# Holding the scores back ahead of the last step of the last input chunk, and transposing the first layer's first queries one step later

## The chip, the cores and the metric

The kernel runs on one core of a Trainium2 chip. The metric is the device time of one execution in microseconds (us). Engines are named as in the profile: PE (TensorE's matmuls), PEld (its weight loads), DVE (VectorE), ACT (ScalarE), POOL (GpSimd), SP (the queue that issues most transfers). "L466" is line 466 of the kernel before; in the changed kernel the same line is a few lines further down.

## The reference

The program is a transformer trunk of two layers, 256 tokens by 2048 features, all in float32. Cut to what matters here:

```python
for l in range(2):
    h = rmsnorm(x, norm_mix[l])
    proj = h @ w_in[l]                       # columns of three mixers: A, B, C
    oa = window_attention(qa, ka, va, ...)       # 8 heads, 2 kv heads, +-128 tokens, sink, bias
    ob = neighborhood_attention(qb, kb, vb, ...) # 8 heads, 2-D window, bias
    oc = axial_global_attention(qc, kc, vc, ...) # 16 heads, 4 kv heads, rotary, all tokens
    mix = concat(rmsnorm(oa, ga), rmsnorm(ob, gb), rmsnorm(oc, gc))
    x = x + mix @ w_o[l]
    h = rmsnorm(x, norm_mlp[l])
    u = relu(h @ w_up[l])
    x = x + (u * u) @ w_down[l]
out = rmsnorm(x, norm_final)
```

## The kernel before, in words

**Steps.** All weight matrices are cut into tiles of 128 x 1024 numbers. One tile is one `Step`. The loop at the end of the kernel goes through the steps in order: it issues the load of a tile seven steps ahead (`load`, on SP, into one of five `wraw` buffers), splits a tile two steps ahead into a rounded high part and a low part (`split`: a cast `whi<-wraw` on ACT, L1013, and a subtraction `wlo<-wraw,whi` on DVE, L1014; each fourth pair goes to buffers called `spare`), runs the step's matmuls (`s.mm`, for the projections L466), and then calls `tick()`.

A step of a projection has three matmuls for each product: high by high, high by low, low by high. A wide input step and an output step are 12 matmuls of 512 columns; a step of the narrow chunk `kva` is 24 of 256 columns.

**Order of the steps.** In each layer the input chunks come as `qa, kva, kvc, qc0, qc1, vb, b0, b1`, eight steps each (`kva` four). Then come the output steps, group by group in the order A, C, B: for A 4 column blocks of 2 steps, for C 4 of 4, for B 4 of 2. Then the MLP follows.

**Evacuation.** After the last step of a chunk `proj_evac` copies the two PSUM banks to SBUF on ACT (for `b0`, `b1` at L515, for `qa` at L565) and queues the pieces that come from it.

**Pieces and units.** Attention is done in pieces that are put between the steps. A unit covers four pairs of head and query block and has three pieces: `unit_scores` (eight matmuls into the score banks `S`, L342 and L343; then on DVE for group C a maximum over the scores, L349, for A and B a fused sum and minimum, L356; on ACT the exponentials, L360; on POOL the reciprocal sums, L369, and four scalings, L371), `unit_transp` (eight transposes, L380, split by ACT, L381, and DVE, L382), and `unit_pv` (matmuls with V, L399 or for group B L392, a copy on ACT, L402, and additions on DVE, L412 or L407). There is one set of score banks. Queries and keys are made ready by `q_transposes` (L255, with copies on ACT, L259, and DVE, L262) and `k_transposes` (L271, with copies and two transfers).

After the last unit of a block, `mix_prep` scales the block for the output projection (ACT L422, DVE L423) and adds its squares on POOL into `sqacc` (L426, then two additions at L435). After the last block of a group, `mix_rs` is queued: a small matmul over `sqacc` (L443) and the reciprocal root (DVE L445, POOL L245). The output steps of a group need that result at the end of their first column block.

**The planner.** `add` puts a piece in the list `bgq` with a cost, the pieces it comes after, and a delay. `tick()` advances a clock `cur` by 2.6, goes through the list, and emits each piece whose predecessors are done and whose delay has passed, until a budget of 2.2 is spent. `need` emits pieces from the head of the list until a flag is set. The layer that records the program then places the instructions of neighbouring pieces and steps into each engine's own list, and picks the buffers; each engine works its list strictly in order.

Of the kernel before, what the change touches and what calls it, by code (L numbers as in the profile page):

```python
# [43 lines left out]
def tile_trunk(ctx: ExitStack, tc: tile.TileContext, x_in, xt_in, w_in, w_o, w_up, w_down,  # L44
# [2 lines left out]
    LOOK_LOAD, LOOK_SPLIT, LOOK_PREP, BUDGET = 7, 2, 5, 2.2  # L47
    N_WARM = 8
    D_X, D_S, D_SS, D_T, D_PV, D_QK, D_RQ, D_RK, D_SQ, D_R = 6.0, 6.0, 7.0, 18.0, 6.0, 6.0, 24.0, 16.0, 6.0, 4.0

    cp = ctx.enter_context(tc.tile_pool(name="cp", bufs=1))
    wp = ctx.enter_context(tc.tile_pool(name="wp", bufs=1))
# [103 lines left out]
    last_lo, last_act, last_load = [None], [None], [None]  # L156

    class Piece:
        pass

    def add(fn, cost, after=(), delay=0, front=False):

        p = Piece()
        p.fn, p.cost, p.after, p.delay, p.at, p.done = fn, cost, after, delay, cur[0], None
        bgq.insert(0 if front else len(bgq), p)
        return p

    def emit(p):
        bgq.remove(p)
        cur[0] += p.cost  # L170
        p.done = cur[0]
        p.fn()

    def tick():
        cur[0] += 2.6
        spent = 0.0
        for p in list(bgq):
            if spent and spent + p.cost > BUDGET:
                break
            if any(q.done is None for q in p.after):  # L180
                continue
            t0 = max([q.done + d for q, d in zip(p.after, p.delay)]) if p.after else p.at + p.delay
            if t0 <= cur[0]:
                emit(p)
                spent += p.cost
# [142 lines left out]
    def queue_unit(u, *preps):  # L328

        after = list(preps) + last_s[-1:]  # L330
        sc = add(lambda: unit_scores(u), 0.87, after=after, delay=[D_S] * len(preps) + [D_SS])
        tr = add(lambda: unit_transp(u), 0.87, after=(sc,), delay=(D_T,))
        add(lambda: unit_pv(u), 0.87, after=(tr,), delay=(D_PV,))
        last_s.append(sc)

    def unit_scores(u):
# [36 lines left out]
    def unit_transp(u):  # L373
        u.ph = big(F32R, 2, 512)
        u.pl = big(F32R, 2, 512)
        for kb in range(2):
            ps = tr_bank()
            for s in range(4):
                c = u.col(s)
                nc.tensor.transpose(ps[:, c * P:(c + 1) * P], u.p[:, s, kb * P:(kb + 1) * P], ident)  # L380
            nc.scalar.copy(u.ph[:, kb, :], ps)  # L381
            nc.vector.tensor_sub(u.pl[:, kb, :], ps, f(u.ph[:, kb, :]))  # L382
# [68 lines left out]
    steps = []  # L451

    class Step:


        def __init__(self, src, kk, n, pre, mm, fourth=True, loads=None, prep=None, raw=None, post=None):
            self.src, self.kk, self.n, self.pre, self.mm, self.fourth = src, kk, n, pre, mm, fourth
# [28 lines left out]
    def layer_steps(l):  # L486
        st = {"hT": [None] * 8, "ss": small(8 if l else 4), "mixT": [None] * 8, "sqacc": {}, "rg": {}, "V": {}, "q": {}, "k": {}}
# [22 lines left out]
        def proj_evac(name, banks):  # L510
            r = st["r"]
            if name in ("b0", "b1"):
                qs = big(F32, NT, 512)
                for t in range(NT):
                    nc.scalar.activation(qs[:, t, :], banks[t], AF.Copy, scale=r[:, t:t + 1])  # L515
                qT, kh, kl = big(F32R, 4, 256), big(F32R, 4, 256), big(F32R, 4, 256)
                pq = add(lambda: q_transposes(qs, 0, qT, 0.125), 0.45, delay=D_QK)
                i = int(name[1])
                pk = add(lambda: k_transposes(qs, 2, 2, kh, kl), 0.45, after=(pq,), delay=(2.6,))
                for u in range(2):  # L520
                    queue_unit(b_unit(l, st, 4 * i + 2 * u, qT, kh, kl), pq, pk)
            elif name == "vb":
                V = [big(F32R, NT, 4, 2, 64) for _ in range(2)]
                st["V"]["B"] = V
                for t in range(NT):
                    v_split(banks[t], [(0, 4, V[0]), (256, 4, V[1])], t, r[:, t:t + 1])
            elif name == "kvc":
                raw = mid(F32, NT, 4, 64)
                V = big(F32R, NT, 4, 2, 64)
                st["V"]["C"] = V  # L530
                for t in range(NT):
                    nc.scalar.activation(raw[:, t].rearrange("p h d -> p (h d)"), banks[t][:, 0:256], AF.Copy,
                                         scale=r[:, t:t + 1])
                    v_split(banks[t], [(256, 4, V)], t, r[:, t:t + 1])
                ks = mid(F32, NT, 256)

                def outs(t, a, b):
                    nc.gpsimd.tensor_add(ks[:, t, :].rearrange("p (h d) -> p h d", h=4), a, b)
                rope(raw, 4, "k", l, outs)
                kh, kl = big(F32R, 4, 256), big(F32R, 4, 256)  # L540
                st["k"]["C"] = (kh, kl)
                st["kC"] = add(lambda: k_transposes(ks, 0, 2, kh, kl), 0.45, delay=D_RK)
            elif name in ("qc0", "qc1"):
                raw = big(F32, NT, 8, 64)
                for t in range(NT):
                    nc.scalar.activation(raw[:, t].rearrange("p h d -> p (h d)"), banks[t], AF.Copy,
                                         scale=r[:, t:t + 1])
                qs = big(F32, NT, 512)

                def outs(t, a, b):  # L550
                    nc.gpsimd.tensor_add(qs[:, t, :].rearrange("p (h d) -> p h d", h=8), a, b)
                rq = rope(raw, 8, "q", l, outs)
                i = int(name[2])
                kh, kl = st["k"]["C"]
                for g in range(2):
                    qT = big(F32R, 4, 256)
                    pq = add(lambda g=g, qT=qT: q_transposes(qs, 2 * g, qT, 1.0), 0.45, delay=D_RQ)
                    for qb in range(2):
                        c0 = qb * 8 + 4 * g
                        queue_unit(g_unit(l, st, "C", 2 * i + g, qb, qT, kh, kl, st["V"]["C"],  # L560
                                          rq=rq[:, c0:c0 + 4]), pq, st["kC"])
            elif name == "qa":
                qs = big(F32, NT, 512)
                for t in range(NT):
                    nc.scalar.activation(qs[:, t, :], banks[t], AF.Copy, scale=r[:, t:t + 1])  # L565
                st["q"]["A"], st["qA"] = [], []
                for g in range(2):
                    qT = big(F32R, 4, 256)
                    st["q"]["A"].append(qT)
                    st["qA"].append(add(lambda g=g, qT=qT: q_transposes(qs, 2 * g, qT, 0.125), 0.45, delay=D_QK))  # L570
            else:
                ks = mid(F32, NT, P)
                V = mid(F32R, NT, 2, 2, 64)
                for t in range(NT):
                    nc.scalar.activation(ks[:, t, :], banks[t][:, 0:P], AF.Copy, scale=r[:, t:t + 1])
                    v_split(banks[t], [(128, 2, V)], t, r[:, t:t + 1])
                kh, kl = mid(F32R, 2, 256), mid(F32R, 2, 256)
                pk = add(lambda: k_transposes(ks, 0, 1, kh, kl), 0.3, delay=D_QK)
                for g in range(2):
                    bias = bias_a(g)  # L580
                    for qb in range(2):
                        queue_unit(g_unit(l, st, "A", g, qb, st["q"]["A"][g], kh, kl, V, bias), st["qA"][g], pk)

        ti = 0
        for name in IN_CHUNKS:
            wide = name != "kva"
            nk = 2 if wide else 4
            nst = NKB // nk
            n = 512 if wide else 256
            box = {}  # L590
            for k in range(nst):
                src = w_in[l, ti]
                ti += 1

                def pre(k=k, nk=nk):
                    need((("mix", l), (k * nk + nk - 1) // 2))

                def mm(wh, wl, k=k, nk=nk, nst=nst, n=n, box=box, name=name):
                    if k == 0:
                        box["b"] = [mm_bank(), mm_bank()]  # L600
                    hts = [halves(st["hT"][(k * nk + i) // 2]) for i in range(nk)]
                    mode_b(box["b"], hts, wh, wl, [(k * nk + i) % 2 for i in range(nk)], k == 0, k == nst - 1, n,
                           lo_last=l == 0 and name == IN_CHUNKS[0], by_block=k == 0)
                    if k == nst - 1:
                        proj_evac(name, box["b"])
                steps.append(Step(src, nk, n, pre, mm))


        st["hT2"], st["ss2"] = [None] * 8, small(8)
        i = 0  # L610
# [439 lines left out]
    for i, s in enumerate(steps):  # L1050
# [31 lines left out]
        if i == 11:  # L1082
            with tc.issue_after(last_lo[0]):
                setup_tables()
        tick()
    assert not bgq


# [121 lines left out]
```

## Time and profile before

| what | value |
|---|---|
| median of 3 runs | 2006.74 us (2006.64 to 2006.88) |
| profiled execution | 2007.62 us, span of its instructions 2005.8 us |
| PE busy | 99% of the span |
| DVE, ACT, POOL busy | 80%, 61%, 17% |
| granted TensorE clock, mean | 0.999 |

The span runs from the first to the last instruction; the profiled execution's own time is 1.8 us longer. Times inside the execution are given in microseconds from the span's start. A timeline row reads: start, duration, engine, line, operation, output and input tiles, count; in brackets, where there is one, the idle time of the engine just before and what ended it. The ends of PE rows are modelled and overlap the next row; starts are what to go by.

### The profile page before, as it was taken

The numbers are of one execution on the slowest core, as the hardware profiler recorded it, in microseconds if no ns is written. First come the engines' busy times: TensorE is split into PE (matmuls) and PEld (weight loads), VectorE is DVE, ScalarE is ACT, GpSimd is POOL, SyncE is SP. The second block draws the span as 40 slices with busy tenths as digits, with TensorE's granted clock in tenths as the row PEclk, the third lists the DMA queues.
The fourth block names the chain that finished last, engine by engine and source line by source line (L and its number), as shares of the span: only waits on it lengthen the run. The fifth ranks groups of instructions, "written<-read, shape, count | busy, mean of one in ns | idle before, by whom it ended". The sixth has DMA issues, their size and how long they took to land.

```text
span 2005.8 us, 28051 instructions
## 1 busy us (share of the span) xinstructions
PE 1992.2 (99%) x10206; PEld 1698.6 (85%) x10206; DVE 1600.0 (80%) x2121; ACT 1216.0 (61%) x1742; POOL 337.8 (17%) x394
## 2 busy tenths in 40 slices
PE   9999999999999999999999999999999999999998
PEld 7888888888888888888888888888888888888887
DVE  6777877878788888888857688777888888888887
ACT  7657756565655656566657677565655556565664
POOL 0674520000000000000008745100000000000000
PEclk9999999999999999999999999999999999999999
DMA  9755655778787787877766465557787776877774
GB/s 338 215 160 158 210 167 190 218 211 239 210 234 212 218 224 207 246 207 235 207 190 197 147 179 196 179 190 215 208 245 215 232 211 208 243 210 237 198 236 144
DMA packets 118838, 420.62 MB, mean 210 GB/s; under 512 B 13571, under 2 KB 15875, under 8 KB 118700
## 3 DMA queue, kind: packets, MB, share of 16 engines
q1 hardware_dynamic: 109052, 384.18, 59.3%
q0 software_dynamic: 9216, 33.56, 10.2%
q8 instruction: 80, 1.31, 0.3%
q10 hardware_dynamic: 432, 1.10, 0.1%
q14 instruction: 58, 0.48, 0.1%
HBM read 412.99 MB, written 2.11 MB: 207 GB/s over the span
## 4 chain that ended last, share of the span: by engine, by line
PE 95%; DVE 1%; DMA 1%; ACT 1%; issue 1%; SPq 0%; POOL 0%; POOLq 0%; DVEq 0%; ACTq 0%
PE mm L466 40%; PE mm L673 23%; PE S L795 13%; PE mm L678 12%; PE mm L795 2%; PE tr L380 1%; DMA wraw<-in_w_in_dram 1%; PE tr L399 1%; PE S L343 1%; PE S L342 1%; PE tr L223 1%; DVE wlo L1014 0%; ACT big L360 0%; PE tr L392 0%; PE tr L255 0%
## 5 line engine op out<-in xcount | busy, mean ns | idle before, releaser
L1014 DVE TENSOR_TENSOR wlo<-wraw,whi 128x1024 fp32r<-128x1024 f32 (+1 forms) x553 | 680.3, 1232 | 241.5 <-ACT whi L1013 238.7
L1013 ACT CAST whi<-wraw 128x1024 fp32r<-128x1024 f32 (+1 forms) x553 | 579.9, 1051 | 453.8 <-PE mm L466 170.8
L466 PE MATMUL mm<-whi,big 128*128 128x512 f32 (+1 forms) x2172 | 613.2, 386 | 0.6 <-ACT whi L1013 0.6
L673 PE MATMUL mm<-big,whi 128*128 128x512 f32 x2048 | 509.5, 391 | 0.0
L466 PEld LDWEIGHTS mm<-whi,big 128*128 128x128 f32 x2172 | 404.4, 188 | 80.2 <-ACT whi L1013 1.6
L673 PEld LDWEIGHTS mm<-big,whi 128*128 128x128 f32 x2048 | 377.6, 188 | 74.5
L466 PE MATMUL mm<-wlo,big 128*128 128x512 f32 (+1 forms) x1086 | 355.5, 384 | 0.0
L678 PEld LDWEIGHTS mm<-big,wlo 128*128 128x128 f32 x2048 | 279.4, 190 | 20.0
L678 PE MATMUL mm<-big,wlo 128*128 128x256 f32 x2048 | 285.6, 282 | 0.0
L466 PEld LDWEIGHTS mm<-wlo,big 128*128 128x128 f32 x1086 | 204.3, 188 | 38.0
L795 PE MATMUL S<-whi,big 128*128 128x512 f32 x768 | 209.1, 394 | 0.0
L781 POOL DMA_DIRECT2D spare<-in_w_down_dram x32 | 28.0, 876 | 745.8 <-DVE wlo L1014 671.2
L795 PEld LDWEIGHTS S<-whi,big 128*128 128x128 f32 x768 | 134.9, 189 | 21.3 <-DVE x L771 1.0
L466 PE MATMUL mm<-spare,big 128*128 128x512 f32 (+1 forms) x606 | 140.2, 380 | 0.0
L466 PEld LDWEIGHTS mm<-spare,big 128*128 128x128 f32 x606 | 108.9, 188 | 20.4
L795 PE MATMUL S<-wlo,big 128*128 128x512 f32 x384 | 118.8, 391 | 0.0
L781 POOL DMA_DIRECT2D big<-in_w_down_dram x32 | 27.7, 866 | 492.4 <-DVE wlo L1014 485.5
L1013 ACT CAST whi<-big 128x1024 fp32r<-128x1024 f32 x64 | 67.2, 1050 | 70.3 <-PE mm L673 50.4
L1013 ACT CAST whi<-side 128x1024 fp32r<-128x1024 f32 x64 | 67.2, 1051 | 65.4 <-PE mm L673 41.2
L1014 DVE TENSOR_TENSOR wlo<-big,whi 128x1024 fp32r<-128x1024 f32 x64 | 78.3, 1224 | 32.7 <-ACT whi L1013 32.6
L1013 ACT CAST whi<-spare 128x1024 fp32r<-128x1024 f32 x64 | 67.4, 1053 | 52.1 <-PE mm L673 40.8
L1014 DVE TENSOR_TENSOR wlo<-spare,whi 128x1024 fp32r<-128x1024 f32 x64 | 78.0, 1219 | 23.9 <-ACT whi L1013 23.8
(158 smaller groups left out, 2100.3 us busy)
## 6 DMA issues: line engine op xcount, KB each, us to landing
wraw<-in_w_up_dram SPq DMA_DIRECT2D x256, 512.0 KB, 4.4
wraw<-in_w_down_dram SPq DMA_DIRECT2D x160, 512.0 KB, 4.1
wraw<-in_w_in_dram SPq DMA_DIRECT2D x119, 512.0 KB, 3.7
wraw<-in_w_o_dram SPq DMA_DIRECT2D x64, 512.0 KB, 3.7
side<-in_w_down_dram SPq DMA_DIRECT2D x64, 512.0 KB, 4.4
spare<-in_w_down_dram SPq DMA_DIRECT2D x32, 512.0 KB, 4.5
spare<-in_w_down_dram POOLq DMA_DIRECT2D x32, 512.0 KB, 5.8
big<-in_w_down_dram POOLq DMA_DIRECT2D x32, 512.0 KB, 6.5
```

The source lines that it names most:

```text
L223: nc.tensor.transpose(psv[:, kk, t, :], x[:, t, c0:c0 + P], ident)
L342: nc.tensor.matmul(o, st, u.kh[:, kh, :], start=True, stop=False)
L343: nc.tensor.matmul(o, st, u.kl[:, kh, :], start=False, stop=True)
L380: nc.tensor.transpose(ps[:, c * P:(c + 1) * P], u.p[:, s, kb * P:(kb + 1) * P], ident)
L399: nc.tensor.matmul(ps, u.V[:, kb, u.kv, :, :], pt[:, kb, :], start=n == 0, stop=n == 3)
L466: nc.tensor.matmul(banks[t][:, 0:n], a, (wl if part == "hl" else wh)[:, i, :], start=first and i == 0 and part == "hh", stop=last and i == ...
L673: nc.tensor.matmul(box["b"][fs], wh[:, kk, fs * P:(fs + 1) * P], ht, start=s == 0 and kk == 0, stop=False, skip_group_check=True)
L678: nc.tensor.matmul(box["b"][fs][:, 0:256], wl[:, kk, fs * P:(fs + 1) * P], ht[:, 0:256], start=False, stop=s == 3 and kk == 3, skip_group_ ...
L781: nc.gpsimd.dma_start(tile, src(par, j, h).rearrange("p (k n) -> p k n", k=2), accum_op=ALU.add)
L795: nc.tensor.matmul(o, ops[i][a], w[:, i, :], skip_group_check=True, start=fresh and h == 0 and i == 0 and a == 0 and w is wh, stop=h == 1 ...
L1013: last_act[0] = nc.scalar.copy(h[:, part], w[:, part]).ins
L1014: last_lo[0] = nc.vector.tensor_sub(lo[:, part], w[:, part], f(h[:, part])).ins
```

## The change

There are two edits. A tick that is followed by the last step of the last input chunk (`b1`, in both layers) skips all `unit_scores` pieces; they stay in the list for the next tick. And in the first layer alone the two `q_transposes` pieces of `qa` get a delay that is longer by 2.6, which is one step.

```diff
+    STEP = 2.6
...
     class Piece:
-        pass
+        scores = False
...
-    def tick():
+    def tick(hold):
+
         cur[0] += 2.6
         spent = 0.0
         for p in list(bgq):
             if spent and spent + p.cost > BUDGET:
                 break
-            if any(q.done is None for q in p.after):
+            if any(q.done is None for q in p.after) or hold and p.scores:
                 continue
...
         add(lambda: unit_pv(u), 0.87, after=(tr,), delay=(D_PV,))
+        sc.scores = True
         last_s.append(sc)
...
     class Step:
+        alone = False
...
-                    st["qA"].append(add(lambda g=g, qT=qT: q_transposes(qs, 2 * g, qT, 0.125), 0.45, delay=D_QK))
+                    st["qA"].append(add(lambda g=g, qT=qT: q_transposes(qs, 2 * g, qT, 0.125), 0.45,
+                                        delay=D_QK + (l == 0) * STEP))
...
                 steps.append(Step(src, nk, n, pre, mm))
+        steps[-1].alone = True
...
-        tick()
+        tick(i + 1 < len(steps) and steps[i + 1].alone)
```

What this does to the engines' lists shows at three places. The first is PE near the start of layer 0, between the second and the third step of `kva` (`whi_329`, `whi_335` are the first two tiles of `kva`, `tr_392` is a small table product, `big_359` holds the first queries). Before:

```order
L466 MATMUL mm_367<-whi_329,big_148 128x256
L147 MATMUL tr_392<-oh,t5x 8x512
L255 MATMUL tr_396<-ident,big_359 128x128 x4
L255 MATMUL tr_405<-ident,big_359 128x128 x4
L466 MATMUL mm_366<-whi_335,big_161 128x256
```

and now:

```order
L148 MATMUL tr_392<-oh,t5x 8x512
L470 MATMUL mm_366<-whi_335,big_161 128x256
L470 MATMUL mm_367<-whi_335,big_186 128x256
L257 MATMUL tr_426<-ident,big_359 128x128 x4
L257 MATMUL tr_435<-ident,big_359 128x128 x4
L470 MATMUL mm_366<-whi_398,big_210 128x256
```

The eight transposes of the queries stand behind the second step of `kva` instead of ahead of it.

The second place is ACT around the end of `b1` (`mm_1922` and `mm_1923` are the banks of `b1`; `S_2188` before and `S_2230` now are the scores of the same unit, the last one of group C). Before:

```order
L381 CAST big_2172<-tr_2181 128x512
L1013 CAST spare_2365<-wraw_2126 128x1024
L360 ACTIVATE big_2197,sm_2199<-S_2188,sm_2198,rq_1346 128x256 x4
L515 ACTIVATE big_2230<-mm_1922,sm_345 128x512
L515 ACTIVATE big_2230<-mm_1923,sm_345 128x512
L402 COPY ot_2279<-tr_2274 64x512
```

and now:

```order
L384 CAST big_2172<-tr_2181 128x512
L519 ACTIVATE big_2206<-mm_1922,sm_345 128x512
L519 ACTIVATE big_2206<-mm_1923,sm_345 128x512
L1019 CAST spare_2365<-wraw_2126 128x1024
L363 ACTIVATE big_2239,sm_2241<-S_2230,sm_2240,rq_1346 128x256 x4
L405 COPY ot_2279<-tr_2274 64x512
```

The copies of `b1`'s banks now stand ahead of that unit's exponentials; on PE that unit's eight score matmuls have gone from ahead of `b1`'s last step to behind it.

The third place is some 35 us later, where the last unit of group C ends (`sqacc_1820` collects the squares of group C; `S_2580` before and `S_2562` now are the scores of the first unit of `b1`). On POOL before:

```order
L426 TENSOR_TENSOR mid_2560<-mid_2421 128x512
L435 TENSOR_TENSOR sqacc_1820<-sqacc_1820,mid_2560 128x256 x2
L369 TENSOR_TENSOR sm_2600<-sm_2591,mone 128x4
L371 TENSOR_SCALAR big_2589<-big_2589,sm_2600 128x256 x4
L245 TENSOR_TENSOR sm_2663<-sm_2661,mhalf 128x2
```

and now:

```order
L429 TENSOR_TENSOR mid_2604<-mid_2421 128x512
L372 TENSOR_TENSOR sm_2582<-sm_2573,mone 128x4
L438 TENSOR_TENSOR sqacc_1820<-sqacc_1820,mid_2604 128x256
L374 TENSOR_SCALAR big_2571<-big_2571,sm_2582 128x256 x4
L438 TENSOR_TENSOR sqacc_1820<-sqacc_1820,mid_2604 128x256
L247 TENSOR_TENSOR sm_2663<-sm_2661,mhalf 128x2
```

The second addition into `sqacc` now stands behind the reciprocals and the four scalings of the first `b1` unit. On DVE the additions that make `mid_2421` stood five rows ahead of that unit's scores before:

```order
L412 TENSOR_TENSOR mid_2421<-tr_2526,ot_2531 64x2x128 x2
L631 SCALAR_TENSOR_TENSOR x<-mm_2512,sm_1426,x 128x512
L631 SCALAR_TENSOR_TENSOR x<-mm_2513,sm_1426,x 128x512
L423 SCALAR_TENSOR_TENSOR big_2555<-mid_2421,gn,big_2555 128x256 x2
L1014 TENSOR_TENSOR spare_2668<-wraw_2486,spare_2667 128x1024
L382 TENSOR_TENSOR big_2565<-tr_2573,big_2564 128x512
L356 ISA big_2589,sm_2590<-S_2580,big_2236 128x256
```

and stand behind them now:

```order
L1020 TENSOR_TENSOR spare_2668<-wraw_2470,spare_2667 128x1024
L385 TENSOR_TENSOR big_2547<-tr_2555,big_2546 128x512
L359 ISA big_2571,sm_2572<-S_2562,big_2212 128x256
L415 TENSOR_TENSOR mid_2421<-tr_2590,ot_2595 64x2x128 x2
L426 SCALAR_TENSOR_TENSOR big_2599<-mid_2421,gn,big_2599 128x256 x2
L1020 TENSOR_TENSOR wlo_2728<-wraw_2506,whi_2727 128x1024
```

The small matmul over `sqacc` (L443 before, L446 now) has kept its place on PE, behind the second output step of group C. Layer 1 has the same two moves at the end of `b1` and the same lists around `sqacc`.

## The prediction

> **What bounds the kernel now.** I read the page first, then what PE waited for, then PE's timeline at those waits.
>
> ```profile
> PE 1992.2 (99%) x10206; PEld 1698.6 (85%) x10206; DVE 1600.0 (80%) x2121; ACT 1216.0 (61%) x1742; POOL 337.8 (17%) x394
> ```
>
> PE is the bound: 99% of the span is matmul, so time can only be won where PE stands still, and is lost at once where a new wait holds it. The list of PE's waits (total us, times, longest) has two groups on the queries' transposes, and beside them little more than the start:
>
> ```profile
> PE tr L255 <- ACT big L515: 2.3, 2, 1.1
> ...
> PE tr L255 <- ACT big L565: 1.2, 2, 1.0
> ```
>
> So some 3.5 us are idle at just the two places that the change touches: behind `qa` in layer 0 (L565), and behind `b1` in both layers (L515). The matmul ends are modelled, so I take the real loss from starts.
>
> **First edit in time: the first queries.** PE behind `qa`, and the two operands that matter on ACT and DVE:
>
> ```profile
> 31.49 1.02 PE L147 MATMUL tr<-oh,t5x 33*8 33x512 f32 x2
> 33.49 0.33 PE L255 MATMUL tr<-ident,big 128*128 128x128 f32 x1 [0.98 <-ACT big L565]
> 34.07 0.98 PE L255 MATMUL tr<-ident,big 128*128 128x128 f32 x7 [0.25 <-ACT big L565]
> 34.81 0.36 PE L466 MATMUL mm<-whi,big 128*128 128x256 f32 x1
> 40.65 3.04 PE L466 MATMUL mm<-spare,big 128*128 128x256 f32 x24
> 43.53 0.40 PE L466 MATMUL mm<-whi,big 128*128 128x512 f32 x1
> ...
> 32.75 1.26 ACT L565 ACTIVATE big<-mm,sm 128x512 f32<-128x512 f32 x2 [0.30 <-POOL sm L245]
> ...
> 30.41 1.23 DVE L1014 TENSOR_TENSOR wlo<-wraw,whi 128x1024 fp32r<-128x1024 f32 x1 [3.45 <-ACT whi L1013]
> ```
>
> From 31.49 to 40.65 are 9.16 us. The work in them: L147, 0.86 (its 1.02 less the 0.16 by which a PE row outlasts the next start); eight transposes, 0.87 (below); two steps of 24 at 43.53 - 40.65 = 2.88, so 5.76. Together 7.49; 1.67 us are lost. In the changed order the second `kva` step comes first. Its low part is done at 30.41 + 1.23 = 31.64, ahead of the 32.35 at which PE is free. The transposes then come at 32.35 + 2.88 = 35.23, and ACT finished the queries at 34.01. Nothing holds them: **-1.67** (bounds: the idle of the rows alone, 1.23, to all of it).
>
> **Second edit: the end of `b1`.** PE from the transposes ahead of `b1`'s last step (204.35) to the second output step:
>
> ```profile
> 202.52 1.03 PE L380 MATMUL tr<-ident,big 128*128 128x128 f32 x8
> 203.31 0.36 PE L342 MATMUL S<-big,big 128*128 128x256 f32 x1
> ...
> 204.35 2.91 PE L466 MATMUL mm<-spare,big 128*128 128x512 f32 x12
> 207.09 0.39 PE L466 MATMUL mm<-whi,big 128*128 128x512 f32 x1
> ...
> 209.81 1.07 PE L399 MATMUL tr<-big,big 128*128 128x512 f32 x4
> 210.72 0.39 PE L466 MATMUL mm<-whi,big 128*128 128x512 f32 x1
> ...
> 212.47 0.33 PE L255 MATMUL tr<-ident,big 128*128 128x128 f32 x1 [1.13 <-ACT big L515]
> ...
> 215.27 1.03 PE L380 MATMUL tr<-ident,big 128*128 128x128 f32 x8
> ```
>
> A step is 2.74 (207.09 - 204.35), eight transposes 0.79 and 0.08 on the first row behind them. From 210.72 to 215.27 are 4.55; a step and four transposes are 2.72 + 0.43, so 1.40 are lost. Why is seen on ACT and DVE:
>
> ```profile
> 205.57 1.07 ACT L381 CAST big<-tr 128x512 fp32r<-128x512 f32 x2
> ...
> 209.54 0.56 ACT L360 ACTIVATE big<-S,sm,rq 128x256 f32<-128x256 f32 x1 [1.15 <-DVE sm L350]
> ...
> 211.72 1.27 ACT L515 ACTIVATE big<-mm,sm 128x512 f32<-128x512 f32 x2
> ```
>
> The four exponentials (209.54 to 211.72) stand ahead of the copies. In the new list the copies follow L381, so they end near 206.64 + 1.27 = 207.9, 2.8 ahead of the transposes at 210.72. The wait goes in both layers, since the row of windows for the same piece of layer 1 reads alike (length, PE busy):
>
> ```profile
> 203.31:215.27 11.96, 10.83 (x56) 8.70 (x55) 8.42 (x13) 10.03 (x20) 9.01 (x12) 1.00 0.71 236
> 1199.02:1210.98 11.96, 10.81 (x55) 8.66 (x54) 8.44 (x13) 10.03 (x20) 9.02 (x12) 1.00 0.69 234
> ```
>
> **-2.80** in all. The moved scores' own work on PE is unchanged. On SP one `w_o` load now stands behind three `side` loads, and they wait for POOL additions that have moved ahead, not back; a later one waits for `wlo_2397`, which DVE reaches later, but its tile is split only some steps on. I cost these at nothing; what hides them is the run of four or more output steps of 2.74.
>
> **What is late next.** Holding the scores moves the later pieces too. The last unit of C gives its values (`mid_2421`) one step later, and POOL's second addition into `sqacc` is now behind the first `b1` unit's reciprocals and scalings. L443 on PE waits for that addition, at the same place in PE's list:
>
> ```profile
> 238.41 0.36 PE L342 MATMUL S<-big,big 128*128 128x256 f32 x1
> ...
> 245.87 0.55 PE L443 MATMUL tr<-full,sqacc 128*128 128x64 f32 x4
> ...
> 239.03 1.04 POOL L426 TENSOR_TENSOR mid<-mid 128x512 f32<-128x512 f32 x1
> 240.14 1.73 POOL L435 TENSOR_TENSOR sqacc<-sqacc,mid 128x256 f32<-128x256 f32 x2
> ```
>
> Before, POOL had finished at 241.87, 4.0 ahead of PE. Now PE, 1.4 earlier (in the clock of the trace, without the gain in layer 0), comes to L443 at 244.5. When is POOL done? The unit's scores on DVE come first, and DVE is full on the way there:
>
> ```profile
> 213.63:244.08 30.45, 30.45 (x161) 25.90 (x160) 30.19 (x52) 21.20 (x41) 17.97 (x23) 1.00 0.62 208
> ...
> 213.63 0.85 DVE L412 TENSOR_TENSOR mid<-tr,ot 64x256 f32<-64x256 f32 x2 [2.98 <-ACT ot L402]
> ...
> 239.93 1.35 DVE L423 SCALAR_TENSOR_TENSOR big<-mid,gn,big 128x256 fp32r<-128x256 f32 x2
> ...
> 244.08 0.41 DVE L356 CUSTOM_DVE_ANT_0 big<-S,big 128x256 f32<-128x256 f32 x1
> ```
>
> DVE is busy for 30.19 of the 30.45 us from 213.63 to that unit's L356. By the order, the same instructions stand there now less one L412 pair (0.85) and one L423 pair (1.35), and the start is 0.2 earlier, as L402 no longer follows the copies. So L356 begins at 213.45 + 30.45 - 2.20 = 241.7; if rows that ran slow beside POOL run freely, down to 240.3. I take 241.0. Then, by rows:
>
> ```profile
> 246.69 1.02 POOL L369 TENSOR_TENSOR sm<-sm,mone 128x4 f32<-128x4 f32 x1 [4.81 <-ACT big L360]
> ...
> 225.56 1.84 POOL L371 TENSOR_SCALAR big<-big,sm 128x256 f32<-128x256 f32 x4
> ...
> 235.16 3.90 POOL L371 TENSOR_SCALAR big<-big,sm 128x256 f32<-128x256 f32 x4
> ...
> 234.12 3.69 DVE L1014 TENSOR_TENSOR wlo<-wraw,whi 128x1024 fp32r<-128x1024 f32 x3
> ```
>
> L369 follows L356 by 2.61 (246.69 - 244.08), so the reciprocals could run at 243.6. But L426 stands ahead of them and needs DVE's L412, which now follows four L356 (1.37): 241.0 + 1.37 + 0.85 = 243.2. L426 then takes 1.11 (240.14 - 239.03), L369 1.1, one addition 0.86, four scalings 1.84 when DVE leaves POOL alone and 3.90 beside three L1014, the other addition 0.86. Two L1014 stand on DVE there, so I take 3.2 for the scalings and 0.3 more on an addition: 243.3 + 1.11 + 1.1 + 0.86 + 3.2 + 0.86 + 0.3 = 250.7. PE stands still from 244.5 for some **6.2 us in each layer**. Ends: L356 at 240.3 with free scalings and additions, 3.9; L356 at 241.7, half a microsecond between L412 and L426 and slow scalings, 8.0.
>
> [...]
>
> **The clock after the stall.** PE's start, and its last matmul against the granted clock at the end (the third number from the right of a row of windows):
>
> ```profile
> 1.63 3.78 PE L1025 MATMUL mm<-warm 128*128 128x512 f32 x8 [1.63 <-DVE warm L1020]
> 5.28 1.66 PE L466 MATMUL mm<-whi,big 128*128 128x512 f32 x4
> ...
> 1996.98 0.88 PE L466 MATMUL mm<-spare,big 128*128 128x256 f32 x6
> ...
> 2003.00:2004.00 1.00, 0.00 (x0) 0.00 (x0) 0.00 (x0) 0.00 (x0) 0.00 (x0) 0.57 1.02 418
> ```
>
> In the last row the clock reads 0.57: it fell to half 5.3 us after PE's last end at 1997.86. At the start eight matmuls took (5.28 - 1.63)/8 = 0.46 each instead of 0.23, and four more 0.37: up to 2.4 us lost on a cold restart. A stall of 6.2 passes the 5.3 by little, so I take 1.3 for each layer, over the middle of 0 and 2.4.
>
> [...]
>
> **Sum.** -1.67 - 2.80 + 2 x 6.2 + 2 x 1.3 = +10.5. The profiled execution took 2007.62 and would take 2018.1; the median shown is 0.88 under it, so 2006.74 + 10.5 = **2017.3 us**.
>
> **Rivals.**
> - *The clock stays up.* The stall is there, but PE is back before the clock falls (under 5.3) or the restart is free: -4.47 + 12.4 = +7.9, 2014.7. For it: only one fall is on record, at 5.3. 0.20.
> - *The wait is hidden and the change is faster.* If POOL ended both additions by 244.5, the three gains stand alone: 2006.74 - 4.47 = 2002.3. For it: POOL is busy for 17% of the span only. Against it: L356 would have to begin at 241.0 - 6.2 = 234.8, ahead of its own score matmuls (PE, 238.41 before, less 1.4 and less an L399 group of 0.91 that now follows them, 236.1). 0.06.
> - *A short stall.* At under 4.2 us a layer with no clock loss the sum stays within 4.0 us of before: about 2008. It needs a DVE that is over 1.5 us quicker. 0.09.
> - *More waits than seen*, such as one on `wlo_2397`, which on DVE has moved behind four L356: 2 us more in each layer would give 2021.3. 0.03.
>
> **How the numbers follow.** The likeliest case has 0.62, with its own range 2012 to 2022. No change within 0.2% (4.0 us) is about what a measurement of this kernel can tell from none. Low end: stalls of 4.2 and no clock loss, 2006.74 - 4.47 + 8.4 = 2010.7. High end: 7.4 and full clock loss, -4.47 + 14.8 + 4.8 = +15.1, 2021.9. Outside lie the faster case, most of the short stall and the last rival. Faster 0.06, same 0.09, slower 0.85.
>
> **What would show it.** PE's waits lose both L255 groups and gain the sqacc matmul on POOL, twice, 3.9 to 8.0 us each, near 243 and 1236; POOL shows L426, L369, one addition, scalings, one addition. A granted clock under 1.00 right behind them shows the clock term; if it stays 1.00, that term is wrong. If PE's list of waits is empty, the DVE walk is wrong.

## The result and the profile after

The change made the kernel slower. The changed kernel takes 2022.48 us (median of 5 runs, 2022.33 to 2024.93), the kernel before 2006.74 us (5 runs, 2006.64 to 2007.47): a ratio of 1.0080, with a 95% interval of 1.0067 to 1.0093. The prediction was 2017.3 us with a range that ended at 2021.9. The direction and the place of the loss were right; the size was 5 us short, and the stall's length, which agrees, agrees by luck (below).

The profiled execution after took 2024.93 us, with a span of 2023.2 us and a mean clock of 0.995. Line numbers are 2 to 6 higher than before: L466 is L470, L443 is L446, L392 is L395, L380 is L383, L435 is L438, L371 is L374, L356 is L359, L412 is L415, L1014 is L1020. First PE's waits (total us, times, longest):

```profile
PE tr L446 <- POOL sqacc L438: 11.9, 2, 5.9
PE mm L470 <- DVE wlo L1020: 1.7, 2, 0.8
...
```

Both groups of waits on the queries' transposes are gone, as the diff intends. In their place stands the small matmul over `sqacc`, once in each layer, and a wait on a weight's low part that was not there before. The rest of the list lies in the first 12 us, where PE waited 1.7 us for casts of weights, 0.6 before. PE's timeline after, at the places of the prediction:

```profile
32.26 1.02 PE L148 MATMUL tr<-oh,t5x 33*8 33x512 f32 x2
...
39.93 3.04 PE L470 MATMUL mm<-spare,big 128*128 128x256 f32 x24
...
201.89 1.03 PE L383 MATMUL tr<-ident,big 128*128 128x128 f32 x8
...
213.33 1.04 PE L383 MATMUL tr<-ident,big 128*128 128x128 f32 x8
...
223.42 0.50 PE L470 MATMUL mm<-wlo,big 128*128 128x512 f32 x1 [0.82 <-DVE wlo L1020]
...
244.29 1.11 PE L395 MATMUL tr<-big,big 128*128 128x256 f32 x8
251.34 1.11 PE L446 MATMUL tr<-full,sqacc 128*128 128x64 f32 x4 [5.94 <-POOL sqacc L438]
...
259.55 2.91 PE L470 MATMUL mm<-spare,big 128*128 128x512 f32 x12
...
1249.29 1.11 PE L395 MATMUL tr<-big,big 128*128 128x256 f32 x8
...
1263.86 2.91 PE L470 MATMUL mm<-spare,big 128*128 128x512 f32 x12
```

In layer 1 PE started L446 at 1256.34, 7.05 us behind L395 as in layer 0. The rows of the kernel before that answer to the last five, as far as the prediction has not shown them:

```profile
244.91 1.12 PE L392 MATMUL tr<-big,big 128*128 128x256 f32 x8
...
250.88 2.91 PE L466 MATMUL mm<-spare,big 128*128 128x512 f32 x12
...
1240.62 1.12 PE L392 MATMUL tr<-big,big 128*128 128x256 f32 x8
...
1246.59 2.91 PE L466 MATMUL mm<-spare,big 128*128 128x512 f32 x12
```

From these starts the change can be read stretch by stretch (us; each is the difference of two starts in one trace):

| stretch on PE | before | after | predicted | measured |
|---|---|---|---|---|
| L147 to the third `kva` step (first queries) | 9.16 | 7.67 | -1.67 | -1.49 |
| end of `b1`: L380 to the next L380, layer 0 | 12.75 | 11.44 | -1.40 | -1.31 |
| from there to L392, layer 0 | 29.64 | 30.96 | 0 | **+1.32** |
| L392 to the step behind the stall, layer 0 | 5.97 | 15.26 | +7.5 | **+9.29** |
| the same, layer 1 | 5.97 | 14.57 | +7.5 | **+8.60** |

Between the two stalls (250.88 to 1240.62 before, 259.55 to 1249.29 after) both kernels take 989.74 us: layer 1's gain at `b1` too is given back ahead of its stall. The rows sum to +16.4; the start is 0.8 later in this execution, and the spans differ by 17.4. The median is 2.45 us under this execution, so the sizes hold for it and not for each run.

The clock behind the two stalls, in windows cut where it changes (length, then busy time and count of PE, PEld, DVE, ACT and POOL, then granted clock, DMA share and GB/s):

```profile
245.00:247.74 2.74, 0.40 (x4) 0.20 (x2) 2.46 (x4) 2.40 (x4) 2.74 (x3) 1.00 0.00 0
247.74:251.34 3.60, 0.00 (x0) 0.00 (x1) 1.90 (x3) 0.00 (x0) 3.55 (x6) 0.50 0.70 204
251.34:257.99 6.65, 6.65 (x19) 5.38 (x20) 0.16 (x1) 0.23 (x1) 0.71 (x1) 0.50 0.12 47
...
1256.34:1261.50 5.16, 5.16 (x14) 4.29 (x15) 0.16 (x1) 0.00 (x0) 0.71 (x1) 0.50 0.20 80
```

PE works for 6.65 us in layer 0 and 5.16 us in layer 1 at half clock. PE came to L446 at 245.25 (L395 and 0.96 for its eight matmuls), so the stall itself is 6.09 us in each layer; the rest, 9.29 - 6.09 = 3.20 and 8.60 - 6.09 = 2.51, is the slow clock.

### The profile page after: what moved, and what is told of

Its sections match the earlier page's. It is cut to its first block, busy times and chain, and to the rows that moved or that the text cites. A ratio compares the mean times of both kernels' runs of the same rounds, so it can differ in the third digit from the quotient of the medians.

```text
span 2023.2 us, 28066 instructions
## 1 busy us (share of the span) xinstructions
PE 1998.4 (99%) x10206; PEld 1703.2 (84%) x10206; DVE 1601.3 (79%) x2121; ACT 1214.7 (60%) x1742; POOL 339.3 (17%) x394
## 3 DMA queue, kind: packets, MB, share of 16 engines
q8 instruction: 80, 1.31, 0.3%
## 4 chain that ended last, share of the span: by engine, by line
PE 94%; DVE 3%; issue 1%; ACT 1%; POOL 1%; DMA 1%; SPq 0%; POOLq 0%; DVEq 0%; ACTq 0%
PE mm L470 39%; PE mm L679 23%; PE S L801 13%; PE mm L684 12%; PE mm L801 2%; PE tr L383 1%; PE tr L402 1%; DVE wlo L1020 1%; PE S L346 1%; PE S L345 1%; DVE big L385 1%; PE tr L225 1%; ACT big L363 0%; DMA wraw<-in_w_in_dram 0%; DVE spare L1020 0%
## 5 line engine op out<-in xcount | busy, mean ns | idle before, releaser
L1020 DVE TENSOR_TENSOR wlo<-wraw,whi 128x1024 fp32r<-128x1024 f32 (+1 forms) x553 | 681.8, 1235 | 248.8 <-ACT whi L1019 245.3
L470 PE MATMUL mm<-whi,big 128*128 128x512 f32 (+1 forms) x2172 | 617.1, 387 | 1.7 <-ACT whi L1019 1.7
L470 PEld LDWEIGHTS mm<-whi,big 128*128 128x128 f32 x2172 | 406.2, 189 | 83.1 <-ACT whi L1019 2.8
L470 PE MATMUL mm<-wlo,big 128*128 128x512 f32 (+1 forms) x1086 | 357.2, 385 | 1.7 <-DVE wlo L1020 1.7
L470 PEld LDWEIGHTS mm<-wlo,big 128*128 128x128 f32 x1086 | 205.5, 189 | 40.9 <-DVE wlo L1020 2.5
L470 PE MATMUL mm<-spare,big 128*128 128x512 f32 (+1 forms) x606 | 140.4, 381 | 0.0
L470 PEld LDWEIGHTS mm<-spare,big 128*128 128x128 f32 x606 | 108.9, 188 | 20.4
L1020 DVE TENSOR_TENSOR wlo<-big,whi 128x1024 fp32r<-128x1024 f32 x64 | 78.4, 1225 | 32.9 <-ACT whi L1019 32.8
L1020 DVE TENSOR_TENSOR wlo<-spare,whi 128x1024 fp32r<-128x1024 f32 x64 | 78.1, 1221 | 24.1 <-ACT whi L1019 24.0
```

What stands on the lines that cost most here:

```text
L470: nc.tensor.matmul(banks[t][:, 0:n], a, (wl if part == "hl" else wh)[:, i, :], start=first and i == 0 and part == "hh", stop=last and i == ...
L1020: last_lo[0] = nc.vector.tensor_sub(lo[:, part], w[:, part], f(h[:, part])).ins
```

## The experiments

The theory: the loss is PE standing behind POOL's second addition into `sqacc`, which is late because DVE is full on the way there, and the clock that falls in that stall. The rivals: the loss comes of the first queries, or it is not tied to that place and moves on when it is taken away there.

**The later queries alone** (`e1_queries_alone`).

```diff
-        tick(i + 1 < len(steps) and steps[i + 1].alone)
+        tick(False)
```

> Only the later first queries are kept; no scores are held back. Theory (each edit is worth what its own place shows): PE loses its wait behind `qa` and nothing else moves, 1.5 us by the starts (9.16 less 7.67), so about 2005.2 us, and the wait behind `b1` in both layers and the sqacc order are those of before. Rival (what PE gains early is taken back at a later wait on DVE or on a load): about 2006.7 us, no change.

Measured: 2007.34 us against 2007.19 of before on the same chip, ratio 1.0003 (0.9994 to 1.0012). So the loss isn't here, but neither is the gain: the rival's number was right. Its mechanism, a later wait, isn't in this run's own trace; there ACT began to copy the queries at 31.60, 1.2 us earlier than in the trace before, so there was little to gain. The two next runs say why.

**Scores held back alone** (`e2_hold_alone`): `delay=D_QK` again, without the `STEP`.

> Only the scores are held back; the first queries stay where they were before. Theory: the whole loss is in this edit, and the 1.5 us of the queries are missing, so about 2024.0 us (2022.5 + 1.5), with PE's two waits for POOL's sqacc at 6 us each. The phase of the clock's fall against the stall is open, which gives 2 us either way. Rival (the loss comes of both edits together, through the start of layer 0 that moved): clearly below 2020 us.

Measured: 2023.24 us, ratio 1.0079 (1.0067 to 1.0092), with two sqacc waits of 5.9 us: the whole loss. That it isn't 1.5 us above the full change shows in its start, where the queries stand as in the kernel before. The first three rows are ACT and PE of this run, the last one ACT of the kernel before (its copies of the queries, at 32.75, are in the prediction):

```profile
26.73 1.16 ACT L201 ACTIVATE big<-x,zero 128x1024 f32<-128x1024 f32 x1 [0.82 <-DMA x<-in_x_dram]
...
31.53 1.26 ACT L569 ACTIVATE big<-mm,sm 128x512 f32<-128x512 f32 x2 [0.29 <-POOL sm L247]
...
32.59 1.24 PE L257 MATMUL tr<-ident,big 128*128 128x128 f32 x8
```

```profile
27.77 1.15 ACT L199 ACTIVATE big<-x,zero 128x1024 f32<-128x1024 f32 x1 [2.07 <-DMA x<-in_x_dram]
```

Here the transfer of `x` landed 1.0 us earlier, the copies of the queries began 1.2 us earlier, and PE doesn't wait for them. Five traces have the queries where they stood before: three show PE's wait for them (1.2 us before, 1.3 in `e9_exps_later`, 0.5 in `e10_exps_split`), two show none (this one and `e8_hold_sum`). So the wait in the profile before is not a fixed property of the order; it goes with a late `x`.

**Queries with and without the delay, stall taken away** (`e8_hold_sum` is `e6_sum_on_pe` below, without the `STEP`).

> The scores held back and group C's last sum on PE, but the first queries where they were before the change. Compared with the same kernel with the later queries (2009.45 us), it tells what the later queries do. Theory (they are worth nothing on the median: PE reaches the first scores earlier than the keys' transfer lands, and waits there 0.5 to 2.1 us instead): the same or up to 1.5 us faster, 2008 to 2009.5 us, a narrower spread, and no wait of the first scores for a transfer. Rival (the later queries are worth their 1.5 us in each run): about 2011 us.

Measured: 2009.08 us, against 2009.45 with the delay (both 1.001 of before): the delay is worth nothing that can be measured, as the theory said. The expected reason failed in part, though: without the delay too PE waited here for the keys' transfer, 1.1 us at L346.

The eight traces with the delay put this wait in an order. Where ACT had waited 0.4 to 0.8 us ahead of its third square of `x` (the row at 27.77 in the kernel before), PE waited 0, 0, 0 and 0.5 us for the keys; where ACT had waited 1.4 to 1.9 us, PE waited 0.8, 1.7, 1.9 and 2.1 us. So in those executions in which the delay spares PE a wait for the queries, PE waits for the keys instead. That both waits go back to a late `x` is argued from this order only, and the run here (0.4 us for `x`, 1.1 for the keys) doesn't fit it; what makes the keys' transfer late wasn't separated.

**The sum taken off POOL** (`e6_sum_on_pe`).

```diff
-            for kk in range(2):
-                nc.gpsimd.tensor_add(acc, acc, sq[:, kk, :])
+            if grp != "C" or blk != GROUP_BLOCKS[grp][-1]:
+                for kk in range(2):
+                    nc.gpsimd.tensor_add(acc, acc, sq[:, kk, :])
...
-            add(lambda: mix_rs(l, grp, acc, done), 0.45, delay=D_SQ)
+            parts = [acc] + [sq[:, kk, :] for kk in range(2) if grp == "C"]
+            add(lambda: mix_rs(l, grp, parts, done), 0.45, delay=D_SQ)
...
+            for j, a in enumerate(acc):
+                nc.tensor.matmul(ps[:, t * 64:(t + 1) * 64], a[:, t * P:(t + 1) * P], full[:, 0:64],
+                                 start=j == 0, stop=j == len(acc) - 1)
```

> The change, with group C's last two additions into sqacc taken off POOL: the small matmul sums acc and the two halves of the squares in PSUM (eight more matmuls of 64 columns). L429 on POOL is then the last that it waits for, and that ended at 245.0 in the trace after the change, where PE comes at 245.3. Theory (the whole loss is POOL's second addition standing behind the scalings, and the clock that falls behind that stall): no wait, no cold stretch, 2022.5 - 2 x 6.1 - 2 x (2.0 to 3.1) + 2 x 0.3 = 2005 to 2007 us; the first queries bring nothing on the median, so the start counts as before. Rival (as in the kernel with the matmul moved back, PE is held by DVE or ACT a few steps further on): 2012 us or more.

Measured: 2009.45 us, ratio 1.0012 (1.0003 to 1.0021), between the 2005 to 2007 of the theory and the 2012 of the rival; the changed kernel on the same chip took 2023.69. PE at the place of the stall:

```profile
244.44 1.12 PE L395 MATMUL tr<-big,big 128*128 128x256 f32 x8
245.40 0.33 PE L449 MATMUL tr<-full,sqacc 128*128 128x64 f32 x2
...
251.30 2.91 PE L474 MATMUL mm<-spare,big 128*128 128x512 f32 x12
```

No wait and no fall of the clock: L395 to the next marked step is 6.86 us in place of 15.26 (5.97 before; the eight added matmuls cost 0.89, not the 0.3 that was expected). Taking that one dependence away removes 14.2 of the 16.4 us by which the changed kernel's median stood above 2007.28. This is the main test, and the stall does not move on. What is left above the kernel before is where it was: PE still waits for the low part ahead of the sum (in layer 0, 31.02 us from the end of `b1` to L395, 29.64 before), and the eight matmuls come on top.

**The changed kernel again, on that chip** (`after_again`).

> The changed kernel once more, on the same chip as the three others, for their comparison and for a second trace of its start and of its two stalls. About 2022.5 us; two sqacc waits of 5.9 us; clock at 0.50 behind each, for two or three stretches of 3.4 us.

Measured: 2023.69 us (2022.47 to 2026.08), ratio 1.0082 (1.0068 to 1.0096), sqacc waits of 6.0 and 5.9 us; the clock read 0.50 behind both.

**The stall filled with work** (`e4_stall_filled`).

```diff
+        if grp == "C":
+            for _ in range(20):
+                nc.tensor.matmul(ps, warm[:, 0:P], warm, start=True, stop=True)
```

> The change, with 20 matmuls of 512 columns on a constant tile added ahead of group C's small matmul, into the bank that it overwrites: PE works for some 4.6 of the 6.1 us that it otherwise stands still. Theory (2.5 to 3.2 us of each stall's price are the clock that fell behind it): POOL's end is where it was, the clock stays at 1.00, and 2 x 2.5 to 3.2 us go: about 2017 us. Rival (the clock's fall costs nothing, since the work behind the stall waits for DVE anyway): 2022.5 us, and more if the added matmuls reach over POOL's end.

Measured: 2019.50 us, ratio 1.0062 (1.0050 to 1.0075). PE's rows, and the clock from the stall on:

```profile
243.99 1.11 PE L395 MATMUL tr<-big,big 128*128 128x256 f32 x8
244.94 4.71 PE L447 MATMUL tr<-warm 128*128 128x512 f32 x20
251.05 0.66 PE L449 MATMUL tr<-full,sqacc 128*128 128x64 f32 x4 [1.40 <-POOL sqacc L438]
...
256.18 2.91 PE L473 MATMUL mm<-spare,big 128*128 128x512 f32 x12
```

```profile
245.00:251.05 6.05, 4.65 (x22) 3.51 (x21) 4.06 (x6) 2.09 (x3) 5.99 (x7) 1.00 0.39 106
251.05:258.00 6.95, 6.95 (x40) 6.09 (x41) 2.48 (x4) 2.53 (x4) 0.71 (x1) 1.00 0.18 64
```

POOL ends where it did, and the clock stays at 1.00. L395 to the marked step is 12.19 us: 3.07 less than after the change, and 6.22 more than before, which is the stall by itself. So the slow clock alone costs 3 us there. On the same chip `e2_hold_alone`, whose stalls are not filled, took 2023.24 us: filling them gains 3.7 us, or 1.9 a layer, less than the 5.4 us expected. Between the traces of these two the same stretch is 2.4 us shorter in layer 0 and 2.0 in layer 1; 0.8 us of this profiled execution went to the keys' transfer (above).

**The sum placed later** (`e3_sum_later`): `mix_rs` of group C gets `delay=40.0` in place of `D_SQ`.

> The change, with the small matmul over group C's sqacc (L446) queued so that PE comes to it only behind C's first column block, some four steps later; POOL's order is unchanged. Theory (the loss is PE standing behind POOL's second sqacc addition, and the slow clock that follows): both stalls (2 x 6.1 us) and both cold phases (2 x 2.5 to 3.2 us) go, 2022.5 - 12.2 - 5.4 = about 2005 us. Rival (DVE or POOL are late as a whole and PE waits for them at the next place instead): a wait of like length further on, 2015 us or more.

Measured: 2019.60 us, ratio 1.0060 (1.0047 to 1.0072): a miss, and a flawed test. At the old place PE passes without a stall. But `need` takes pieces from the head of the list until the sum is there, so it pulled the transposes and products of group B together, and L395 waits 2.6 us for ACT's L384 and 1.1 us for DVE's L385. A later L446 waits 0.8 us for POOL's `sqacc` in each layer. The run can't tell whether the loss moves on of itself.

**The weight's low part earlier** (`e5_split_early`), so that PE doesn't wait for `wlo_2397`.

```diff
+                with tc.issue_after(last_lo[0]) if wlo_first[0] else nullcontext():
+                    nc.vector.tensor_tensor_reduce(p[:, s, :], S[:, s, :], ...)
...
-        while ns < min(len(steps), i + LOOK_SPLIT + (not s.fourth)):
+        while ns < min(len(steps), i + LOOK_SPLIT + (not s.fourth) + 2 * (i >= 2 and steps[i - 2].alone)):
...
+        wlo_first[0] = i >= 2 and steps[i - 2].alone
```

> The change, with the weight tile whose low part PE waits for in the third column block (`wlo_2397`) split two steps earlier and kept ahead of the first scores on DVE behind `b1`, as before the change. Theory (DVE is full from there to the scores of the first `b1` unit, so POOL ends no earlier): PE's wait for wlo goes, 0.8 us twice, and the wait for sqacc grows by as much: unchanged against the change, 22.5 us within 1 (2021.5 to 2023.5). Rival (that wait is on the path by itself): 2 x 1.0 to 1.3 us faster, about 2020 us.

Measured: 2024.02 us, ratio 1.0082 (1.0068 to 1.0096), the same as the change on that chip (2023.69).

```profile
214.74 0.49 PE L384 MATMUL tr<-ident,big 128*128 128x128 f32 x3
...
244.87 1.11 PE L396 MATMUL tr<-big,big 128*128 128x256 f32 x8
252.85 1.11 PE L447 MATMUL tr<-full,sqacc 128*128 128x64 f32 x4 [6.87 <-POOL sqacc L439]
```

The wait for wlo is gone and the stall is 0.9 us longer. From the end of `b1` (214.74) to the sum are 38.11 us, after the change 251.34 - 213.33 = 38.01: DVE and POOL set that time, and PE's wait for the low part on the way costs nothing while the stall is there.

**Both** (`e7_both`: the sum on PE and the earlier split).

> Both edits together: the sum on PE and the earlier split. Theory: with the stall gone the wait for wlo counts by itself, so this is 2 x 0.8 to 1.2 us faster than the sum on PE alone, about 2003 to 2005 us, and the fastest of these. Rival (DVE's fullness makes PE wait at the next place in any case): no faster than the sum on PE alone.

Measured: 2009.27 us, no better than the sum alone; the theory failed here and its rival held. With the wait for wlo gone PE comes earlier and waits 0.4 to 0.5 us for POOL's L430 (L429 in the changed kernel) instead. This trace also holds a short stall that cost clock: PE waited 2.08 us for the keys' transfer and began again at 58.72:

```profile
58.72:59.97 1.25, 1.25 (x9) 1.21 (x10) 0.14 (x1) 0.00 (x0) 0.00 (x0) 0.99 0.52 206
59.97:63.39 3.42, 3.42 (x10) 2.64 (x9) 2.78 (x10) 2.08 (x8) 0.00 (x0) 0.51 0.02 6
```

The clock was half for some 3.4 us, from about 1.2 us after PE had begun again.

**Only the exponentials later** (`e9_exps_later`, from the kernel before). The gain at `b1` needs ACT's copies ahead of one unit's exponentials, not the unit one step later.

```diff
+        def rest():
             for s in range(4):
                 nc.scalar.activation(p[:, s, :], src[s], AF.Exp, ...)
             ...
+        if late[0]:
+            add(rest, 0.0, front=True)
+        else:
+            rest()
...
+        late[0] = i + 1 < len(steps) and steps[i + 1].alone
         tick()
```

> The kernel before, in which only the exponentials (with what follows them) of the unit ahead of the last step of `b1` are recorded one step later; its score matmuls and maxima stay where they were, so ACT copies the banks of `b1` first, and no later unit moves. Theory (what the change removes at `b1` is worth 1.3 us in each layer, and all its loss is the later units): PE's waits for L515 go, POOL's additions into sqacc stand ahead of the reciprocals as before, no stall; 2 x 1.3 us less at `b1`, 2 x 0.8 of it given back at wlo_2397, which DVE again reaches behind four scores: about 2005.5 us against 2007.2. Rival (any delay of these exponentials delays the chain to sqacc by as much): a stall of some 1 to 3 us in each layer, 2008 us or more.

Measured: 2005.81 us against 2007.29, ratio 0.9991 (0.9982 to 1.0000): 1.5 us faster, at the edge of its interval. PE's rows at the end of `b1` and at the sum:

```profile
204.48 1.03 PE L385 MATMUL tr<-ident,big 128*128 128x128 f32 x8
...
215.90 1.04 PE L385 MATMUL tr<-ident,big 128*128 128x128 f32 x8
...
246.01 1.12 PE L397 MATMUL tr<-big,big 128*128 128x256 f32 x8
246.97 0.55 PE L448 MATMUL tr<-full,sqacc 128*128 128x64 f32 x4
```

The stretch at the end of `b1` is 11.42 us (12.75 before), from there to the sum's transposes 30.11 (29.64), and L448 follows without a wait, since POOL's additions stand where they stood. That is 0.9 us a layer, 1.7 in all, where 1.7 was expected; the part given back is not a wait for wlo, though, but small steps on the way. Of all the kernels here this one and the next are the fastest. The profiled execution was the slowest of its eleven (2007.84 us), with slow matmuls at its start (last section).

**The same with the earlier split** (`e10_exps_split`).

> The same with the tile of wlo_2397 split two steps earlier, and kept ahead of the scores on DVE. Theory: the gain at `b1` is kept whole, 2 x 1.3 us less than before, about 2004.5 us, no wait for wlo. Rival (DVE is full there, so the low part that comes earlier makes the next work late): no better than without it.

Measured: 2005.72 us, ratio 0.9992 (0.9984 to 1.0001): no better than without, as the rival said. There was no wait for wlo to take away, and a new one came (two keys' transposes wait for DVE, 0.5 us each).

## Why the prediction came out short

Four terms were off. Most of the miss is in two of them: the moment at which DVE begins its walk to the stall (under "The stall"), and the clock.

- **First queries, -1.67.** In the trace -1.49, so the reading of the rows was right. On the median it is nothing (1.0003, with an interval that excludes the whole gain but leaves room for up to 1.2 us). The step that failed is "1.67 us are lost": it took one execution's wait for a fixed cost, and didn't follow it back to what ended it, the transfer of `x` ahead of ACT's squares. This misses 1.7 us.
- **End of `b1`, -2.80.** Measured -1.31 in layer 0, and `e9_exps_later` shows that it can be had. But the step "what hides them is the run of four or more output steps" costed the low part at nothing. It cost PE 0.82 us of idle. From the end of `b1` to L395 are 30.96 us now, 30.13 in `e5_split_early` without that wait, and 29.64 before; the other 0.49 us are small steps that no run traces to a cause. So PE reached the sum no earlier than before.
- **The stall, 6.2 in each layer.** Measured 6.09, but by two errors that cancel, which is luck. PE came 1.4 us later than predicted (the line above), and POOL was done 1.3 us later too: L446 started at 251.34, which is 251.97 in the clock of the trace before (L380 at 202.52 there, L383 at 201.89 here), where 250.7 was predicted. The step that failed is "the start is 0.2 earlier, as L402 no longer follows the copies". DVE before, at the maxima of the unit that the change holds back:

```profile
208.10 1.21 DVE L349 TENSOR_REDUCE sm<-S 128x4 f32<-128x1024 f32 x1
209.34 0.16 DVE L350 TENSOR_TENSOR sm<-sm,rq 128x4 f32<-128x4 f32 x1
```

  and ACT, DVE and POOL after:

```profile
205.89 1.28 ACT L519 ACTIVATE big<-mm,sm 128x512 f32<-128x512 f32 x2
...
211.34 0.56 ACT L363 ACTIVATE big<-S,sm,rq 128x256 f32<-128x256 f32 x1 [3.23 <-DVE sm L353]
...
213.66 0.58 ACT L405 COPY ot<-tr 64x512 f32<-64x512 f32 x1
...
207.47 1.22 DVE L352 TENSOR_REDUCE sm<-S 128x4 f32<-128x1024 f32 x1
208.60 1.82 DVE L1020 TENSOR_TENSOR spare<-wraw,spare 128x1024 fp32r<-128x1024 f32 x1
210.34 0.90 DVE L353 TENSOR_TENSOR sm<-sm,rq 128x4 f32<-128x4 f32 x1
214.27 0.85 DVE L415 TENSOR_TENSOR mid<-tr,ot 64x256 f32<-64x256 f32 x2 [3.03 <-ACT ot L405]
...
241.71 0.41 DVE L359 CUSTOM_DVE_ANT_0 big<-S,big 128x256 f32<-128x256 f32 x1
...
207.49 4.63 POOL L970 TENSOR_TENSOR big<-side,cs 128x384 f32<-128x384 f32 x4
```

  The copies do move ahead, and L405 (L402 before) no longer follows them. But it stands behind the held unit's exponentials, and these wait for the small product L353 (L350 before), which scales the unit's maxima on DVE. The maxima began at the same moment as before (207.47 is 208.10 in the clock of before), although the scores came 2.8 us later on PE. Before, the product followed them at once. Now the subtraction L1020 of a weight tile stands between the two, and beside POOL's additions L970 it took 1.82 us (1.23 before, in the row behind L350) and the product 0.90 instead of 0.16. So the exponentials began 2.4 us later than before, L405 1.3 us later, and DVE's L415, for which DVE stood idle for 3.0 us, at 214.27 (214.90 in the clock of before, predicted 213.45), 1.5 us later than predicted. Layer 1 and `e2_hold_alone` have the same rows with the same times within 0.02 us. No run put the product back ahead of that subtraction, so its price is read from the rows, not tested.

  From L415 to L359 DVE took 27.4 us (predicted 27.5), and the walk on POOL from L359 to its end 9.6 us (predicted 9.7):

```profile
244.00 1.04 POOL L429 TENSOR_TENSOR mid<-mid 128x512 f32<-128x512 f32 x1 [6.74 <-DVE mid L415]
245.00 1.20 POOL L372 TENSOR_TENSOR sm<-sm,mone 128x4 f32<-128x4 f32 x1
246.18 1.63 POOL L438 TENSOR_TENSOR sqacc<-sqacc,mid 128x256 f32<-128x256 f32 x1
247.80 2.80 POOL L374 TENSOR_SCALAR big<-big,sm 128x256 f32<-128x256 f32 x4
250.57 0.72 POOL L438 TENSOR_TENSOR sqacc<-sqacc,mid 128x256 f32<-128x256 f32 x1
```

  The order is the one predicted, row for row. The first addition took 1.63 us and the four scalings 2.80 us beside two L1020, the scalings between the 1.84 of the row before that ran beside L278 and L412 on DVE and the 3.90 of the row beside three L1014; 3.2 was taken. DVE was busy beside the row of 1.84 too; the rows show how long the scalings took and what ran beside them, not why they differ. The larger part of the stall is POOL's order: with both additions right behind L429, as before the change, they would have ended near 245.1 + 1.7 = 246.8, some 1.6 us behind PE (an estimate from L435's 1.73 before). No run changed that order alone. Each layer lost 6.1 us net of the gain and without the clock, where 6.2 - 1.4 = 4.8 was predicted: 2.6 us for two layers.
- **The clock, 1.3 in each layer (bounds 0 and 2.4).** Measured 3.20 and 2.51 in the trace, above the upper bound. The bound was the program's own start, where eight matmuls took 0.46 us each and four 0.37 in place of 0.23 (the granted clock reads 1.00 there; that it made them slow is not shown); here it read 0.50 for 6.65 and 5.16 us of PE's work. This term, the one that was mis-sized most, misses 3.1 us in this execution. Three more traces have both stalls; reckoned in the same way the slow clock costs 3.0 and 2.4 us in `after_again`, 2.6 and 2.2 in `e2_hold_alone`, and 1.7 twice in `e5_split_early`, each above 1.3.

In the profiled execution the account closes to 0.1 us: it was predicted at 2018.1 and took 2024.93 us, and of these 6.8 us the queries make 0.2, the two layers 2.6, the clock 3.1 and the later start 0.8, 6.7 in all. On the median, 5.2 us above the prediction, the queries' 1.7 and the layers' 2.6 us leave 0.9 for clock and start together; the executions differ in both (2022.33 to 2024.93), and no trace of the median shows how it divides.

The rival "the clock stays up" is excluded by the clock of 0.50 behind the stalls and by `e4_stall_filled`. Its reason, that the only fall on record came 5.3 us behind PE's last matmul, was one sample: in the four traces with both stalls seven falls, all but the one in layer 1 of `e5_split_early`, came 2.5 to 5.4 us behind it. The rival "more waits" was right about the place, `wlo_2397`, and wrong about its price: `e5_split_early` shows that the wait costs nothing while the stall is there. Its 2021.3 us also lies inside the range 2010.7 to 2021.9, not outside as the prediction has it.

## What to carry to other kernels

When a piece of work is put one step later, walk its last instruction, not its first, and on each queue look for what now stands between its parts. Here a subtraction between two small steps on DVE held the exponentials on ACT, these held a copy, and the copy held DVE again; DVE was full for the next 27 us (busy for 27.02 of the 27.44 from L415 to L359) and could not make it good, and an engine that is busy 17% of the time held PE at the end of that chain. To free one queue, move only the instructions that stand in the way (`e9_exps_later`), not the unit they belong to. And before a wait in a profile is counted as a gain, look at what ended it: a wait that hangs on when a transfer lands is not in each execution.

## What the runs showed of the hardware

In the trace after the change the granted clock read 0.50 for a stretch in each layer, from inside the stall on. It fell or rose at 247.74, 257.99, 1254.66 and 1261.50: the low stretches are 10.25 and 6.84 us, and one of 3.42 us stands in `e7_both`. The fall came 2.5 us after PE's last matmul in layer 0, 4.4 us after it in layer 1, and in `e7_both` 1.25 us after PE had begun again behind a wait of 2.08 us. So a stall cost more than its length, and not each time the same: behind two stalls of 6.09 us PE ran at half clock for 6.65 and 5.16 us. What sets the moment of the fall and the length of the low stretch is not shown.

The shortest stop with slow matmuls behind it is at the start of `e9_exps_later`, behind `qa`:

```profile
33.87 0.33 PE L255 MATMUL tr<-ident,big 128*128 128x128 f32 x1 [1.00 <-ACT big L571]
34.45 1.56 PE L255 MATMUL tr<-ident,big 128*128 128x128 f32 x7 [0.25 <-ACT big L571]
```

PE was idle for 1.25 us in two parts. Then the seven transposes took 1.56 us, and from 36.0 to 37.9 the matmuls of 256 columns came some 0.21 us apart, from 38.4 on 0.12; the mean clock of this execution is 0.998. In the kernel before nearly the same two waits (0.98 and 0.25) cost no clock: the seven transposes took 0.98 us, and from 34 to 39 the clock reads 1.00. Idle time by itself doesn't decide it: in `after_again` the clock fell only at 252.2, when PE had been idle for 5.4 us. What else counts is not shown.
